# Six late conditioning pieces: from weight-column matmuls on TensorE to multiply-adds on VectorE

## The chip, the cores and the metric

The kernel runs on one core of one Trainium2 chip. The metric is the device time of one launch in microseconds (us). Before the change three runs gave 1612.42, 1619.84 and 1621.44 us, with a median of 1619.84 us. Engines are called as in the profile: PE is TensorE (matmuls; PEld its weight loads), DVE is VectorE, ACT is ScalarE, POOL is GpSimd, SP the engine whose queue issues most of the DMAs.

## The reference, cut to what matters

One decoder layer for 512 tokens of width 1024. A conditioning vector `c` (1024 numbers) is turned into six modulation rows of 1024 numbers, and these scale, shift and gate the two halves of the layer:

```python
mod = jax.nn.silu(c) @ w_ada[l] + b_ada[l]                 # (1, 6*1024)
sh_m, sc_m, g_m, sh_f, sc_f, g_f = jnp.split(mod, 6, axis=-1)
h = modulate(rmsnorm(x, norm_g[l, 0]), sh_m, sc_m)
proj = h @ w_in[l]
a_out = nsa_mixer(...)          # three-branch attention, 8 heads of 64, softmax
c_out = conv_mixer(...)         # depthwise convolution, LayerNorm over channels, swish
x = x + g_m * (jnp.concatenate([a_out, c_out], -1) @ w_out[l])
h = modulate(rmsnorm(x, norm_g[l, 1]), sh_f, sc_f)
x = x + g_f * peer_ffn(h, ...)  # product-key retrieval over 16384 experts
```

The product `silu(c) @ w_ada` is a vector times a 1024 x 6144 matrix. All of it is float32. Only `sh_m` and `sc_m` are needed before the projections; the other rows are needed later.

## The kernel before, in words

The product is cut into twelve pieces of 512 columns (`pc` 0 to 11; piece `pc` belongs to modulation row `pc // 2`). The weights of a piece are two halves (`hf` 0 and 1) of 1 MB, each an SBUF tile `wst` of 128 partitions x 4 x 512: four blocks of 128 rows of `w_ada`. There are three `wst` buffers, which also carry other weights. `cs` holds silu(c) as 128 x 8, and `cs32` the same repeated 32 times along the free side.

Before the change (L207 to L225) a half is four matmuls: block `j` of the weights streams through PE against a 32-column copy of one column of `cs`, into 32 partitions of a PSUM tile of its own block. With `hf` 0 and 1 these accumulate. `mod_fin` lets ACT copy 97 partitions of that PSUM tile into the SBUF tile `rows` (whose last partition holds the bias row, loaded by DMA), and a small matmul against a column that selects partitions 0, 32, 64, 96 and 127 adds the four partial rows and the bias. Its result goes by an ACT copy to `modc` (a column form, pieces 6 to 9) or to `gfbc` (a form broadcast over partitions, pieces 10 and 11).

Pieces 6 to 11 are the late ones. They run inside the attention loop, whose index is `i` from 0 to 17. Iteration `i` computes scores for unit `i` (a query tile of 128 tokens and a pair of heads; four score tiles each, `sc_mm`, L663 on PE and L665 on DVE, which adds the position term and takes the row maximum), exponentials for unit `i - 1` (`sc_exp`, ACT), and for unit `i - 2` the transposes (`turn`, L143 on PE, L698 on ACT) and the products with the values (`values`, L705 and L710 on PE). DVE also scales the exponentials of unit `i - 1` (`weigh`, L685 and L690). Query tile `n` is prepared by `prep` one tile ahead, and a LayerNorm over the convolution's channels is spread over iterations 5, 9, 12 and 13. In the table `mit` the pieces start at the iterations 0, 2, 4, 6, 8 and 10.

The order on DVE in this loop is the order in which the code is written (a manual schedule). The orders on PE, ACT, POOL and SP are set by the framework's list scheduler. Each engine takes its instructions strictly in its order. The score tiles have three PSUM buffers (`s`), the transposes two (`pt`), and one buffer (`x`) serves the pieces, the LayerNorm and `prep` in turn. After the last piece `mod_scale(1)` finishes two rows of `modc`, and `wo_load` starts the loads of the output projection's weights into the same three `wst` buffers; `split` casts the first of them on ACT (`wxhi`, L122) and subtracts on DVE (`wxlo`, L114).

Of the kernel before, what the change touches and what calls it, by code (L numbers as in the profile page):

```python
# [9 lines left out]
F32 = mybir.dt.float32  # L10
# [10 lines left out]
P = 128  # L21
S = 512
# [86 lines left out]
def layer(ctx: ExitStack, tc: tile.TileContext, a, out):  # L109
    nc = tc.nc  # L110
    mult, add, sub = ALU.mult, ALU.add, ALU.subtract

    def tt(o, i0, i1, op):
        return nc.vector.tensor_tensor(out=o, in0=i0, in1=i1, op=op)  # L114

    def act(o, i, f, **k):
        return nc.scalar.activation(o, i, f, **k)  # L117
# [16 lines left out]
    ones = cst[:, C_ONE:C_ONE + P]  # L134
    gbc = {}
    gbc["f"] = const.tile([P, D], F32, name="gfbc")
    modc = const.tile([P, 4, 8], F32, name="modc")
# [7 lines left out]
    with ExitStack() as pre:  # L145
        wpool = pre.enter_context(tc.tile_pool(name="wpool", bufs=1, side="right"))
# [42 lines left out]
        cs = ap_.tile([P, 8], F32, name="cs")  # L189
# [4 lines left out]
        rows = [ap_.tile([P, 512], F32, name=f"rows{k}") for k in range(2)]  # L194
# [6 lines left out]
        def mod_load(pc):  # L201
            was = [wpool.tile([P, 4, 512], F32, name="wst", bufs=3) for _ in range(2)]
            for hf in range(2):
                nc.sync.dma_start(was[hf], a["wada"][pc, hf])
            return was

        def mod_mm(hf, mp, was):  # L207
            for j in range(4):
                nc.tensor.matmul(mp[32 * j:32 * j + 32, :], cs32[:, hf * 4 + j, :], was[hf][:, j, :],
                                 start=hf == 0, stop=hf == 1)  # L210

        def mod_fin(pc, mp, tp, rw):
            act(rw[0:97, :], mp[0:97, :], AF.Copy)
            which, half = pc // 2, pc % 2
            bp = tp()
            if which in (2, 5):
                nc.tensor.matmul(bp, cst[:, C_SEL:C_SEL + 1].to_broadcast([P, P]), rw, start=True, stop=True)
                nc.scalar.copy(gbc["m" if which == 2 else "f"][:, half * 512:(half + 1) * 512], bp)
            else:
                w4 = {0: 0, 1: 1, 3: 2, 4: 3}[which]  # L220
                for cc in range(4):
                    nc.tensor.matmul(bp[:, cc:cc + 1], rw[:, cc * P:(cc + 1) * P], cst[:, C_SEL:C_SEL + 1],
                                     start=True, stop=True)
                (nc.vector.tensor_copy if pc < 4 else nc.scalar.copy)(modc[:, w4, half * 4:half * 4 + 4], bp[:, 0:4])

        def mod_row(pc):
            nc.sync.dma_start(rows[pc % 2][P - 1:P, :], a["bada"][pc:pc + 1, :])

        def mod_both(mp, was):
            for hf in range(2):  # L230
                mod_mm(hf, mp, was)
# [13 lines left out]
        was = {2: mod_load(2), 0: mod_load(0)}  # L245
# [16 lines left out]
        def mod_scale(k, hs=slice(0, 8)):  # L262
            sc = modc[:, 2 * k + 1, hs]
            nc.vector.tensor_scalar(sc, sc, 1.0, None, op0=add)
            tt(sc, sc, ngc[:, k, hs], mult)
# [119 lines left out]
        late = list(range(4, 12))  # L385
# [151 lines left out]
        for n in range(2):  # L537
            for l in range(16):
                nc.tensor.matmul(kcps[:64, n, :], pe[n][:, l:l + 1].to_broadcast([P, 64]), wcmp[:, n, l, :],
                                 start=l == 0, stop=False)  # L540
            for l in range(16):
                nc.tensor.matmul(kcps[:64, n, :], ksb[n][:, 2 * l + 1:2 * l + 1010:16], wcmp[:, n, l, :],
                                 start=False, stop=l == 15)
# [109 lines left out]
        def sc_open(u):  # L653
            u["mx"], u["ng"], u["sm"], u["fc"] = (sb.tile([P, 4], F32, name=n, bufs=4) for n in ("mx", "ngm", "sm", "fc"))
            u["st"], u["pT"] = [], []

        def sc_mm(u, it):
            qt, pr = u["qt"], u["pr"]
            nk, nn = (qt + 1) * P, max((qt + 1) * P, 256)
            h, k = 2 * pr + it // 2, 2 * (it % 2) + pr // 2  # L660
            ps = ps_s.tile([P, S], F32, name="s")
            for q in range(2):
                nc.tensor.matmul(ps[:, :nn], u["o"]["qT"][:, h, :], kst[:, q, k, 0:nn], start=q == 0, stop=q == 1)  # L663
            st = sb.tile([P, S], F32, name="st", bufs=16)
            nc.vector.tensor_tensor_reduce(out=st[:, :nk], in0=ps[:, :nk],  # L665
                                           in1=cst[:, C_BASE + 384 - qt * P:C_BASE + 512],
                                           scale=1.0, scalar=-3e38, op0=add, op1=ALU.max,
                                           accum_out=u["mx"][:, it:it + 1])
            u["st"].append(st)
# [6 lines left out]
        def sc_exp(u, it):  # L676
            nk, h = (u["qt"] + 1) * P, 2 * u["pr"] + it // 2
            st = u["st"][it]
            act(st[:, :nk], st[:, :nk], AF.Exp, scale=float(2.0 ** -(h + 1)),
                bias=u["ng"][:, it:it + 1], accum_out=u["sm"][:, it:it + 1])  # L680
# [11 lines left out]
        def turn(u, it):  # L692
            n = u["qt"] + 1
            pt = ps_t.tile([P, 4, P], F32, name="pt")
            for kb_ in range(n):
                transpose(pt[:, kb_, :], u["st"][it][:, kb_ * P:(kb_ + 1) * P])
            pT = sb.tile([P, 4, P], F32, name="pT", bufs=6)
            nc.scalar.copy(pT[:, :n, :], pt[:, :n, :])  # L698
            u["pT"].append(pT)
# [18 lines left out]
        def x_att():  # L718
            return ps_x.tile([P, S], F32, name="x")

        def tr_att():
            return ps_t.tile([P, 512], F32, name="pt")
# [3 lines left out]
        def wo_load():  # L726
            wos.append(wpool.tile([P, ND, 256], F32, name="wst", bufs=3))
            nc.sync.dma_start(wos[-1], a["wout"][len(wos) - 1])

        mods = {}  # L730

        def mod_get():
            if late:
                pc = late.pop(0)
                mods["next"] = pc, mod_load(pc)
                mod_row(pc)

        def mod_do():
            pc, was = mods.pop("next")
            x = x_att()  # L740
            mod_both(x, was)
            mods["fin"] = pc, x

        def mod_end():
            pc, x = mods.pop("fin")
            mod_fin(pc, x, tr_att, rows[pc % 2])
            if late:
                mod_get()
            else:
                mod_scale(1)  # L750
                for _ in range(3):
                    wo_load()

        late_q, todo = [], {}

        def at_it(i, when, f):
            todo.setdefault((i, when), []).append(f)

        N = 4 * NT
        mit = [0, 2, 4, 6, 8, 10]  # L760
        for i in mit:
            at_it(i, "S", mod_do)
            at_it(i, "E", mod_end)
        L = [5, 9, 12]
        at_it(L[0], "S", ln["mu"])
        at_it(L[0], "E", ln["cen"])
# [2 lines left out]
        at_it(L[2], "S", ln["rep"])  # L769
        at_it(L[2], "E", ln["nrm"])  # L770
        at_it(L[2] + 1, "E", ln["fin"])
        mod_get()
        man = ExitStack()
        man.enter_context(tc.manual_schedule(engines={mybir.EngineType.DVE}))
        us, oo = [], [pre0]
        for i in range(N + 2):
            n, pr = i // 4, i % 4
            A = B = C = None
            if i < N:
                if pr == 0:  # L780
                    oT = ps_o.tile([P, 4, P], F32, name="oT")
                    if n + 1 < NT:
                        oo.append(prep(n + 1, tr_att, x_att))
                        o = oo[-1]
                        at_it(i, "E", o["mul"])
                        todo.setdefault((i + 1, "E"), []).insert(0, o["lo"])
                        at_it(i + 2, "S", o["turn"])
                        at_it(i + 2, "E", o["cmm"])
                        at_it(i + 3, "E", o["cmax"])
                        at_it(i + 4, "E", o["csum"])  # L790
                A = dict(qt=n, pr=pr, o=oo[n], oT=oT)
                sc_open(A)
                us.append(A)
            if 0 <= i - 1 < N:
                B = us[i - 1]
            if 0 <= i - 2 < N:
                C = us[i - 2]
            for k in SL:
                if A:
                    sc_mm(A, k)  # L800
                if B:
                    sc_exp(B, k)
            for f in todo.pop((i, "S"), []):
                f()
            if C:
                for k in SL:
                    turn(C, k)
            if A:
                sc_neg(A)
            if B:  # L810
                weigh(B)
            lq, late_q[:] = list(late_q), []
            if C:
                values(C)
            for f in lq + todo.pop((i, "E"), []):
                f()
            if i < N:
                conv_some(8)
            if i == L[0] - 1:
                conv_some(len(convq))  # L820
# [192 lines left out]
        for h in range(H):  # L1013
# [19 lines left out]
            for t2 in range(2):  # L1033
                ps = psR.tile([P, 2, 2, P], F32, name="sc")
                for k in range(2):
                    t = 2 * t2 + k
                    for c in range(2):
                        nc.tensor.matmul(ps[:, k, c, :], qs[c][:, t * P:(t + 1) * P], kt[:, 2 * h + c, :],
                                         start=True, stop=True)
# [296 lines left out]
    for n in range(NTILE - KL):  # L1336
# [7 lines left out]
        while todo and dma_t < rho * pe_t:  # L1344
            c, f = todo.pop(0)
# [34 lines left out]
```

## Time and profile before

| what | value |
|---|---|
| median of three runs | 1619.84 us (1612.42 to 1621.44) |
| the profiled execution's own time | 1614.99 us |
| its span, from the first to the last instruction | 1613.2 us |
| PE busy over the span | 1560.4 us (97%) |
| DVE busy over the span | 1293.1 us (80%) |
| attention iterations 0 to 11 | 178.98 to 265.64 us of the span |
| DVE busy in these | 52.33 of 86.66 us |
| PE busy in these | 85.58 of 86.66 us |

An iteration is bounded here by the starts of the first of its four score tiles on DVE (L665). A busy share is a sum over instructions; matmuls overlap, so that a full PE is one that never stands empty, not one at its peak. In a timeline row the bracket gives the idle time of the engine before the instruction, and what ended it. The granted clock of PE (PEclk) is 1.00 at 2.4 GHz and 0.50 at 1.2 GHz; values between are averages over a stretch.

### The profile page before, as it was taken

The page shows a single profiled execution, that of the slowest core. Times are in us where ns is not written, and L with a number is a line of the kernel's source. Part 1 is how long each engine was busy: PE and PEld are TensorE (multiplying, and loading weights), DVE is VectorE, ACT ScalarE, POOL GpSimd, SP SyncE. Part 2 cuts the span into 40 slices and gives each one's busy share as a digit, 9 for nine tenths or more (in the row PEclk, how much of TensorE's full clock was granted, in tenths as well). Part 3 has the DMA queues.
Part 4 walks back from the last instruction along what each step waited for, and adds up shares of the span by engine and source line. Part 5 has one row for each costly group of instructions (what it writes and reads, how often), then busy time and mean ns, then how long its engine had stood idle before and what let it go on. Part 6 is the DMA issues. An engine that isn't in the chain of part 4 may idle for free.

```text
span 1613.2 us, 24117 instructions
## 1 busy us (share of the span) xinstructions
PE 1560.4 (97%) x9033; PEld 1361.8 (84%) x9033; DVE 1293.1 (80%) x2590; ACT 755.2 (47%) x1234; POOL 323.3 (20%) x266
## 2 busy tenths in 40 slices
PE   5999998999999999999999999998999999999998
PEld 3779766898889999999999899997897888888887
DVE  4698667578989999988888387786788888878887
ACT  4335558634334544778778433233232333333332
POOL 0000000000002232221222044443454322222210
PEclk9999999999999999999999999999999999999999
DMA  8443242244006877888888989998999999999993
GB/s 316 151 154 123 107 155 79 95 159 152 15 27 206 297 256 252 308 321 311 314 317 283 336 323 337 328 320 312 347 320 346 340 352 352 359 344 350 350 366 143
DMA packets 157166, 416.31 MB, mean 258 GB/s; under 512 B 13036, under 2 KB 76268, under 8 KB 147960
## 3 DMA queue, kind: packets, MB, share of 16 engines
q1 hardware_dynamic: 104048, 236.73, 42.1%
q0 software_dynamic: 36864, 134.23, 23.2%
q10 hardware_dynamic: 16136, 43.79, 7.2%
q8 instruction: 71, 1.16, 0.3%
q14 instruction: 47, 0.39, 0.1%
HBM read 368.25 MB, written 45.88 MB: 257 GB/s over the span
## 4 chain that ended last, share of the span: by engine, by line
PE 71%; DVE 16%; DMA 6%; ACT 4%; issue 3%; SPq 0%; ACTq 0%; DVEq 0%
PE va L1327 8%; PE va L1328 8%; PE va L1326 8%; PE u L1070 7%; PE u L1071 7%; PE u L1072 7%; DVE acc L1179 3%; DVE ulo L114 3%; DVE ldg L1171 3%; DMA ld<-in_uT_dram 3%; DMA ld<-in_vn_dram 2%; ACT vhi L122 2%; PE mm L1026 2%; PE mm L1025 2%; PE mm L1027 2%
## 5 line engine op out<-in xcount | busy, mean ns | idle before, releaser
L1070 PE MATMUL u<-h2hi,uhi 128*128 128x384 f32 x1024 | 350.4, 342 | 7.4 <-ACT act L117 7.2
L1072 PE MATMUL u<-h2hi,ulo 128*128 128x384 f32 x1024 | 346.4, 338 | 4.4 <-DVE ulo L114 4.4
L1071 PE MATMUL u<-h2lo,uhi 128*128 128x384 f32 x1024 | 348.4, 340 | 0.0
L1163 POOL DMA_INDIRECT ldg<-in_un_dram,e_i x128 | 159.8, 1248 | 869.4 <-DVE cand L114 504.6
L1326 PE MATMUL va<-vhi,gshi 128*128 128x512 f32 x756 | 295.9, 392 | 5.3 <-ACT gshi L122 3.4
L1327 PE MATMUL va<-vlo,gshi 128*128 128x512 f32 x756 | 296.7, 393 | 1.6 <-DVE vlo L114 1.5
L1328 PE MATMUL va<-vhi,gslo 128*128 128x512 f32 x756 | 296.4, 392 | 0.0
L114 DVE TENSOR_TENSOR vlo<-ld,vhi 128x1024 fp32r<-128x1024 f32 x126 | 154.3, 1224 | 128.0 <-ACT vhi L122 127.9
L122 ACT CAST vhi<-ld 128x1024 fp32r<-128x1024 f32 x126 | 132.3, 1051 | 229.6 <-issue 164.6
L1163 POOL DMA_INDIRECT ldg<-in_vn_dram,e_i x128 | 161.3, 1260 | 362.8 <-DVE acc L1179 321.6
L1070 PEld LDWEIGHTS u<-h2hi,uhi 128*128 128x128 f32 x1024 | 194.5, 190 | 10.4 <-ACT act L117 8.3
L122 ACT CAST uhi<-ld 128x1024 fp32r<-128x1024 f32 x130 | 137.7, 1060 | 133.4 <-PE u L1071 86.2
L1072 PEld LDWEIGHTS u<-h2hi,ulo 128*128 128x128 f32 x1024 | 194.2, 190 | 5.0 <-DVE ulo L114 5.0
L1071 PEld LDWEIGHTS u<-h2lo,uhi 128*128 128x128 f32 x1024 | 194.5, 190 | 1.3
L114 DVE TENSOR_TENSOR ulo<-ld,uhi 128x1024 fp32r<-128x1024 f32 x130 | 158.5, 1221 | 27.7 <-ACT uhi L122 26.3
L1326 PEld LDWEIGHTS va<-vhi,gshi 128*128 128x128 f32 x756 | 142.8, 189 | 35.6 <-ACT gshi L122 3.7
L1327 PEld LDWEIGHTS va<-vlo,gshi 128*128 128x128 f32 x756 | 142.7, 189 | 31.9 <-DVE vlo L114 3.0
L1328 PEld LDWEIGHTS va<-vhi,gslo 128*128 128x128 f32 x756 | 142.7, 189 | 30.7 <-DVE gslo L114 0.9
L1179 DVE SCALAR_TENSOR_TENSOR acc<-ldg,actg,acc 128x1024 f32<-128x1024 f32 x127 | 162.5, 1279 | 0.0
L1171 DVE SCALAR_TENSOR_TENSOR ldg<-ldg,h2n 128x1024 f32<-128x1024 f32 x128 | 155.9, 1218 | 0.0
L122 ACT CAST gshi<-g 128x384 fp32r<-128x384 f32 x128 | 65.1, 509 | 156.7 <-DVE g L114 156.6
L117 ACT ACTIVATE wb<-mm 128x512 f32<-128x512 f32 x96 | 96.1, 1110 | 47.2 <-PE mm L1134 47.1
(317 smaller groups left out, 2502.8 us busy)
## 6 DMA issues: line engine op xcount, KB each, us to landing
ld<-in_uT_dram SPq DMA_DIRECT2D x128, 512.0 KB
ld<-in_vn_dram SPq DMA_DIRECT2D x128, 512.0 KB
wt<-wd SPq DMA_DIRECT2D x17, 1536.0 KB
wst<-in_wada_dram SPq DMA_DIRECT2D x24, 1024.0 KB
wd<-wb ACTq DMA_DIRECT2D x24, 1024.0 KB
spill<-actw ACTq DMA_DIRECT2D x84, 192.0 KB
sp<-spill SPq DMA_DIRECT2D x21, 768.0 KB
wst<-in_win_dram SPq DMA_DIRECT2D x9, 1024.0 KB
```

The lines of the kernel that those rows point to most:

```text
L114: return nc.vector.tensor_tensor(out=o, in0=i0, in1=i1, op=op)
L117: return nc.scalar.activation(o, i, f, **k)
L122: nc.scalar.copy(hi, src)
L1070: nc.tensor.matmul(ps, hi[:, d, :], h2hi[:, d, :TD], start=d == 0, stop=False)
L1071: nc.tensor.matmul(ps, hi[:, d, :], h2lo[:, d, :TD], start=False, stop=False)
L1072: nc.tensor.matmul(ps, lo[:, d, :], h2hi[:, d, :TD], start=False, stop=d == ND - 1)
L1163: nc.gpsimd.indirect_dma_start(out=gst[-1], out_offset=None, in_=a["un" if kind == "u" else "vn"], in_offset=bass.IndirectOffsetOnAxis(ap= ...
L1171: nc.vector.scalar_tensor_tensor(g, g, 1.0, h2n, op0=mult, op1=mult, accum_out=actg[:, k:k + 1])
L1179: nc.vector.scalar_tensor_tensor(acc, g, actg[:, k:k + 1], acc, op0=mult, op1=add)
L1326: nc.tensor.matmul(vac[t][k], ghi[:, ts_], vhi[:, ks], start=f, stop=False)
L1327: nc.tensor.matmul(vac[t][k], ghi[:, ts_], vlo[:, ks], start=False, stop=False)
L1328: nc.tensor.matmul(vac[t][k], glo[:, ts_], vhi[:, ks], start=False, stop=l)
```

## The change: what it does, and the diff

The matmuls of the six late pieces go. Each of the twelve halves becomes four `scalar_tensor_tensor` instructions on DVE: a 128 x 512 block of weights times the per-partition scalar `cs[:, 4*hf+k]`, added to `rows`. After eight of them `rows` holds 128 partial rows, one per partition; beforehand a POOL memset clears it, and the bias row is loaded into its last partition by the same DMA as before. PE then sums over the partitions with a column of ones (four matmuls with one column, or one with 128), and ACT copies the result as before; the ACT copy of the 97 partitions is gone. A queue `modq` holds the steps: four adds, then the load of a further half, after every second half also the sum; one step is taken after each score tile up to iteration 4, two from iteration 5 on. Three halves are loaded ahead.

```diff
-        def mod_do():
-            pc, was = mods.pop("next")
-            x = x_att()
-            mod_both(x, was)
-            mods["fin"] = pc, x
...
+            pc, hf = halves.pop(0)
+            wa, rw = wpool.tile([P, 4, 512], F32, name="wst", bufs=3), rows[pc % 2]
+            nc.sync.dma_start(wa, a["wada"][pc, hf])
+            if hf == 0:
+                nc.gpsimd.memset(rw, 0.0)
                 mod_row(pc)
...
+            def add_in(k):
+                nc.vector.scalar_tensor_tensor(rw, wa[:, k, :], cs[:, 4 * hf + k:4 * hf + k + 1], rw, op0=mult, op1=add)
+
+            modq.extend([lambda k=k: add_in(k) for k in range(4)])
+            if hf == 1:
+                modq.append(lambda: mod_end(pc, rw))
+            modq.append(mod_get)
+
+        def mod_end(pc, rw):
+            which, half = pc // 2, pc % 2
+            bp = tr_att()
+            if which in (2, 5):
+                nc.tensor.matmul(bp, ones, rw, start=True, stop=True)
+                nc.scalar.copy(gbc["m" if which == 2 else "f"][:, half * 512:(half + 1) * 512], bp)
             else:
+                for cc in range(4):
+                    nc.tensor.matmul(bp[:, cc:cc + 1], rw[:, cc * P:(cc + 1) * P], ones[:, 0:1], start=True, stop=True)
+                nc.scalar.copy(modc[:, {3: 2, 4: 3}[which], half * 4:half * 4 + 4], bp[:, 0:4])
+            if pc == 11:
                 mod_scale(1)
                 for _ in range(3):
                     wo_load()
...
-        mit = [0, 2, 4, 6, 8, 10]
-        for i in mit:
-            at_it(i, "S", mod_do)
-            at_it(i, "E", mod_end)
...
+        for _ in range(3):
+            mod_get()
...
+                mod_some(1 if i < 5 else 2)
```

The order of the instructions moves on three engines. DVE in iterations 9 and 10 (`st` is a score tile, `mx` its row maximum, `ngm` the maximum scaled for the exponentials; `rows_99` and `rows_100` are the two `rows` buffers):

```order
 L665 ISA st,mx<-s,cst 128x384
 L665 ISA mx 128x1
+L745 SCALAR_TENSOR_TENSOR rows_99<-wst,cs,rows_99 128x512
 L665 ISA st,mx<-s,cst 128x384
 L665 ISA mx 128x1
+L745 SCALAR_TENSOR_TENSOR rows_100<-wst,cs,rows_100 128x512
 L665 ISA st,mx<-s,cst 128x384
 L665 ISA mx 128x1
+L745 SCALAR_TENSOR_TENSOR rows_100<-wst,cs,rows_100 128x512 x2
 L665 ISA st,mx<-s,cst 128x384
 L665 ISA mx 128x1
+L745 SCALAR_TENSOR_TENSOR rows_100<-wst,cs,rows_100 128x512
```

The adds stand between the score tiles of an iteration, so that the later score tiles, the scaling and everything behind them on DVE come after up to seven adds of the same iteration (iteration 8 has seven; these are the five of iteration 9).

PE in iterations 1 to 3 (`s` are score products, L222 and L760 the sums of piece 6, `qr` the transposes of the next query tile):

```order
 L705 MATMUL oT<-pc,vbl 128x128
-L663 MATMUL s<-kst,qT 128x256
-L222 MATMUL pt<-cst,rows_99 128x1 x4
-L663 MATMUL s<-kst,qT 128x256 x5
-L209 MATMUL x<-wst,cs_97 32x512 x8
-L143 MATMUL pt<-cst,qr 128x128
-L663 MATMUL s<-kst,qT 128x256 x2
-L143 MATMUL pt<-cst,qr 128x128 x7
+L663 MATMUL s<-kst,qT 128x256 x16
+L760 MATMUL pt<-cst,rows_99 128x1 x4
+L143 MATMUL pt<-cst,qr 128x128 x8
```

The eight matmuls of a piece are gone from between the score products, and the sum of a piece comes later, behind the score products of iteration 2.

ACT in iteration 12, where a LayerNorm's activation (`y<-y,cvec`) needs another table of functions, before the change:

```order
L698 COPY pT<-pt 128x384 x2
L117 ACTIVATE st,sm<-st,ngm 128x512 x4
L117 ACT_TABLE_LOAD
L117 ACTIVATE y<-y,cvec 128x512 x4
L641 CAST hhi<-y 128x512 x4
L471 COPY pc<-pt 128x256
L698 COPY pT<-pt 128x384
L117 ACT_TABLE_LOAD
L117 ACTIVATE st,sm<-st,ngm 128x512
```

The same place after it:

```order
L117 ACTIVATE st,sm<-st,ngm 128x512
L698 COPY pT<-pt 128x384
L117 ACTIVATE st,sm<-st,ngm 128x512 x2
L117 ACT_TABLE_LOAD
L117 ACTIVATE y<-y,cvec 128x512 x4
L641 CAST hhi<-y 128x512 x4
L471 COPY pc<-pt 128x256
L117 ACT_TABLE_LOAD
L117 ACTIVATE st,sm<-st,ngm 128x512
```

The fourth exponential of unit 12 has moved behind the LayerNorm's block and its two table loads.

## Rows read from the trace of the kernel before

**Rows 1.** Windows by iteration: length, each engine's busy us (instructions), PEclk, DMA share, GB/s.
```profile
core 0: us, PE busy (x) PEld busy (x) DVE busy (x) ACT busy (x) POOL busy (x), PEclk, DMA share, GB/s
...
189.84:198.14 8.30, 8.30 (x55) 6.72 (x55) 3.93 (x20) 4.94 (x24) 0.00 (x0) 0.79 0.36 146
...
254.55:265.64 11.09, 11.09 (x90) 8.20 (x88) 7.53 (x21) 9.40 (x24) 0.00 (x0) 1.00 0.24 88
sum 86.66, PE 85.58 PEld 58.81 DVE 52.33 ACT 56.75 POOL 0.00; mean PE 7.13 PEld 4.90 DVE 4.36 ACT 4.73 POOL 0.00
```

**Rows 2.** Waits on DVE, iterations 0 to 11: waiter, waited for, total, times, longest.
```profile
DVE st L665 <- PE s L663: 26.9, 14, 4.5
DVE fc L685 <- ACT st L117: 4.3, 2, 2.3
DVE rv L627 <- ACT rv L117: 1.4, 1, 1.4
```

**Rows 3.** The same windows, only the pieces' matmuls (L209): the sum.
```profile
sum 86.66, PE 15.80 PEld 2.87; mean PE 1.32 PEld 0.24
```

**Rows 4.** Groups on ACT and PE: busy us, mean ns, idle before.
```profile
L117 ACT ACTIVATE rows<-x 97x512 f32<-97x512 f32 x6 | 3.5, 590 | 6.3 <-PE x L209 6.3
L222 PE MATMUL pt<-cst,rows 128*128 128x1 f32 x32 | 4.1, 249 | 0.0
```

**Rows 5.** DVE, the convolution's multiply-adds (L379) and a two-operand subtraction: start, length, operation.
```profile
L379 DVE SCALAR_TENSOR_TENSOR y<-up,dww,y x120: 637/732/751, 62.6 to 174.6; 128x482 f32<-128x482 f32 x4, 128x483 f32<-128x483 f32 x4, 128x484 f32<-128x484 f32 x4, 128x485 f32<-128x485 f32 x4
...
109.46 10.41 DVE L379 SCALAR_TENSOR_TENSOR y<-up,dww,y 128x505 f32<-128x505 f32 x16
...
211.55 2.47 DVE L114 TENSOR_TENSOR y<-y,x 128x512 f32<-128x512 f32 x4
```

**Rows 6.** Timeline of DVE: two waits for score tiles, in iterations 3 and 11.
```profile
194.22 0.29 DVE L665 CUSTOM_DVE_ANT_0 st<-s,cst 128x128 f32<-128x128 f32 x1 [4.09 <-PE s L663]
...
259.45 0.56 DVE L665 CUSTOM_DVE_ANT_0 st<-s,cst 128x384 f32<-128x384 f32 x1 [3.39 <-PE s L663]
```

**Rows 7.** PE busy and PEclk in stretches of 3 us.
```profile
192.00:195.00 3.00, 3.00 (x23) 0.89 0.26 107
195.00:198.00 3.00, 3.00 (x16) 0.54 0.01 3
198.00:201.00 3.00, 3.00 (x22) 1.00 0.00 0
...
240.00:243.00 3.00, 3.00 (x15) 0.50 0.00 0
243.00:246.00 3.00, 3.00 (x13) 0.57 0.00 0
```

**Rows 8.** Groups on PE from 239 to 246 us, then from 247 to 257 us.
```profile
L663 PE MATMUL s<-kst,qT 128*128 128x384 f32 x8 | 3.3, 527 | 0.0
L143 PE MATMUL pt<-cst,st 128*128 128x128 f32 x8 | 2.1, 424 | 0.0
...
L663 PE MATMUL s<-kst,qT 128*128 128x384 f32 x8 | 1.9, 363 | 0.0
L143 PE MATMUL pt<-cst,st 128*128 128x128 f32 x12 | 1.7, 277 | 0.0
```

**Rows 9.** Side conditions: POOL group, DMA window, then DVE and ACT timeline around iteration 12.
```profile
L198 POOL MEMSET rows<- 128x512 f32 x2 | 1.0, 524 | 0.3 <-POOLq L1369 0.3
...
183.00:186.00 3.00, 3.00 (x29) 1.00 1.01 415
...
262.20 2.28 DVE L114 TENSOR_TENSOR wxlo<-wst,wxhi 128x2048 fp32r<-128x2048 f32 x1
...
277.06 0.17 DVE L685 RECIPROCAL fc<-sm 128x4 f32<-128x4 f32 x1
...
280.39 0.72 ACT L117 ACTIVATE st<-st,ngm 128x512 f32<-128x512 f32 x1
```

More of the change, by code (lines that the diff above doesn't have):

```diff
@@ L728, in wo_load @@
             nc.sync.dma_start(wos[-1], a["wout"][len(wos) - 1])
-        mods = {}
+        modq, halves = [], [(pc, hf) for pc in late for hf in range(2)]
+        del late[:]
         def mod_get():
-            if late:
-                pc = late.pop(0)
-                mods["next"] = pc, mod_load(pc)
-                mod_row(pc)
-        def mod_do():
-            pc, was = mods.pop("next")
-            x = x_att()
-            mod_both(x, was)
-            mods["fin"] = pc, x
[L744 to L748, printed above, removed]
-            else:
+            if not halves:
+                return
+            pc, hf = halves.pop(0)
[3 more added lines that the diff above has]
+                nc.gpsimd.memset(rw, 0.0)
+                mod_row(pc)
+            def add_in(k):
[10 more added lines that the diff above has]
+                nc.scalar.copy(gbc["m" if which == 2 else "f"][:, half * 512:(half + 1) * 512], bp)
+            else:
+                for cc in range(4):
+                    nc.tensor.matmul(bp[:, cc:cc + 1], rw[:, cc * P:(cc + 1) * P], ones[:, 0:1], start=True, stop=True)
+                nc.scalar.copy(modc[:, {3: 2, 4: 3}[which], half * 4:half * 4 + 4], bp[:, 0:4])
+            if pc == 11:
                 mod_scale(1)
@@ L752, in mod_end, with mod_some @@
                     wo_load()
+        def mod_some(n):
+            for _ in range(n):
+                if modq:
+                    modq.pop(0)()
         late_q, todo = [], {}
@@ L771, in layer @@
         at_it(L[2] + 1, "E", ln["fin"])
-        mod_get()
+        for _ in range(3):
+            mod_get()
         man = ExitStack()
```

## The prediction

> **What bounds the kernel now.** I read the windows first, cut at the attention iterations, because the change touches iterations 0 to 11 alone; what lies before and behind keeps its instructions and moves as a block with the loop's end. In these 86.66 us PE stands empty for about 1 us, while DVE is busy for 52.33 us [rows 1]. So before the change PE sets the pace here, and the next view, who waits for whom, says the same from the other side: DVE waits 26.9 us for score products, 4.3 us for exponentials and 1.4 us for a root, together 32.6 us [rows 2]. DVE's work with the small gaps between dependent instructions is therefore 86.66 - 32.6 = 54.1 us. Third I looked at what the pieces cost PE: 15.80 us over the loop [rows 3]. Last came the timeline, for where DVE's waits lie: not spread evenly, but one of 3 to 4 us in an iteration in which PE has much between two score tiles, as in iterations 3 and 11 [rows 6].
>
> **What the change removes.** PE loses the 15.80 us of piece matmuls [rows 3]. ACT loses six copies of 0.59 us, 3.5 us in all [rows 4]; ACT is busy 56.75 of 86.66 us [rows 1] and is not the bound, so I count this at nothing. The summing matmuls keep their shapes (L222 before, 4.1 us [rows 4], L760 after). PE's own need falls from about 86 to about 70 us.
>
> **What it adds.** DVE gets 12 halves x 4 = 48 multiply-adds over 128 x 512. The trace has the same operation, with the same accumulation on its own output: the convolution's taps. One lasts 0.73 us in the middle of 120, but neighbours overlap, and sixteen in a row take 10.41 us, which is 0.65 us each [rows 5]. Lower bound: a subtraction of 128 x 512, four of which take 2.47 us, hence 0.60 us with the overlap taken off [rows 5]; upper bound: the longest tap alone, 0.751 us. I take 0.65, since it is the same operation: 48 x 0.65 = 31.2 us (28.8 to 36.0).
>
> So DVE's work becomes 54.1 + 31.2 = 85.3 us in a loop that took 86.66 us. This is the main step of the forecast: the waits of DVE are just large enough to hold the adds (32.6 against 31.2), and the pace passes from PE to DVE. If every wait were filled, the loop would be 1.4 us shorter, no more, whatever PE has won.
>
> **What isn't filled.** The adds stand at fixed places in DVE's order, after the score tiles, and the waits are where PE has a long piece of work between two score products. In iteration 3 DVE waits 4.09 us for its second tile [rows 6], and only one add stands before it; the sum of piece 6, about 1 us of PE, comes off this place since it now runs ahead of the transposes. 4.09 - 0.65 - 1 leaves about 2.5 us. Iteration 11 has no add at all, and its PE order is as before: of 3.39 us I keep 3.0. The other 25.1 us of waits fall in iterations with three to seven adds (2.0 to 4.6 us) and I count them as filled; the two waits for exponentials go, as the adds give ACT the time. So 5.5 us remain. Bounds: 0 us, and at the other end 3 us in each of iterations 3, 7, 9 and 11, where PE has the preparation of a query tile or the LayerNorm's sums between two score products: 12 us (the longest single wait before is 4.5 us [rows 2]).
>
> **Where the clock comes in.** In the stretch from 195 to 198 us PE was granted 0.54 and from 240 to 246 us about 0.5, which is the 1.2 GHz level, though PE was never empty there; behind the first of them it was back at 1.00, the 2.4 GHz level [rows 7]. At the low level a score product takes 527 ns instead of 363 and a transpose 424 instead of 277, 1.5 times as long [rows 8]. Without the pieces PE will stand empty for about a quarter of the loop (70 of some 93 us are its need). The Trainium skill, "TensorE: Matmul & The Clock Gate", Part 1, says that the throttled state is the default and that activity releases it; by that rule the removal makes every remaining matmul of the loop slower rather than only removing work, and the trace agrees in so far as the level does change within this loop, while no run yet shows the loop without the pieces. In rows: at the two places that stay PE-bound PE works for about 4.4 us before the awaited tile (iteration 3, 189.84 to 194.22) and 4.9 us (iteration 11, 254.55 to 259.45) [rows 1, 6]; at 1.5 times that costs 2.2 and 2.5 us. Bounds 0 and 4.7 us; I take half, 2.4 us, since one of the two (iteration 3) already was partly slow before at 0.79 [rows 1].
>
> **Side costs, taken at nothing.** Six POOL memsets of 0.52 us [rows 9] run on an idle engine. The clearing, the bias row and the first add of piece `pc + 2` wait for PE's sum of piece `pc`, but 11 steps of the queue lie between, over an iteration. A load of 1 MB takes 2.5 us at 415 GB/s [rows 9] and has eight adds and at least one iteration of lead; if that cover were gone, an add would block DVE and the score tiles behind it for 1 to 3 us each time. `wxlo`, 2.28 us on DVE [rows 9], moves from iteration 11 into iteration 10 before the last score tile; it now waits for a load that starts when an add of iteration 9 frees the buffer and for an ACT cast, which I see in time by about 1 us (up to 2 us lost if not). In iteration 12 the fourth exponential comes behind the LayerNorm's block. Before, the scaling of that unit stood on DVE at 277.06 and the first exponential after the block at 280.39 [rows 9]; DVE will so wait about 3 us there. It costs nothing or up to 1 us, since the transposes of that unit come only in iteration 14, two iterations behind its scores.
>
> **Sum.** 85.3 + 5.5 + 2.4 = 93.2 us against 86.66, that is +6.5 us. On the profiled execution's 1614.99 us this is 1621.5 us. That execution lies below the median of the runs (1619.84) and above the lowest (1612.42); the mean of these four executions is 1617.2, and I set the forecast on it: 1617.2 + 6.5, or 1624 us.
>
> **Rivals.** *DVE and PE in turn, slower.* Each iteration takes the longer of the two engines, and PE runs at the low clock through the loop. Place: the score tiles behind the transposes in iterations 3, 7, 8 and 11; price 85.3 + 12 = 97.3 us, plus up to 4.7 us for the clock: +11 to +15 us, say +13, 1630 us. It decides if PE is at the low level in more than half of the loop or if more than 9 us of DVE's waits for score products stay. For it: waits of up to 4.5 us at single places, three score buffers only. Against it: PE's work drops by a sixth, so that it can run ahead by its order. *The adds fill every wait, no loss.* DVE is then full and the loop takes 83 to 87 us: -4 to +1 us, 1616 us. For it: 32.6 against 31.2 us; against it: iteration 11 without adds. *PE's gain arrives, faster.* A loop shorter by 8 us would need 78.6 - 54.1 = 24.5 us for 48 adds, 0.51 us each, below the 0.60 of the simpler subtraction; 1608 us. Nothing in the rows speaks for it. *The change stalls on its own inputs*, the adds waiting for loads or for the cleared `rows`: six stalls of 2 us, 1636 us; the lead of one iteration speaks against it.
>
> **How the numbers follow.** About 0.5% (8 us) is what a measurement of this kernel can tell from no change. Forecast (+1 to +8 us): 0.46, own range 1618 to 1627. No loss: 0.09. Engines in turn: 0.36. Own inputs: 0.04. Faster: 0.05. So within 0.5%: 0.46 + 0.09 = 0.55; slower: 0.40; faster: 0.05. The range: below, 28.8 us of adds without any wait, 82.9 us, -3.8 us, 1613; above, adds at 0.751 us (36.0 instead of 31.2) on top of the engines in turn with the whole clock term, 106.8 us, +20 us, 1637.
>
> **What would show it.** Right: DVE busy about 84 us over iterations 0 to 11, its waits for score products down from 26.9 to 5 to 9 us, an add about 0.74 us long at steps of 0.65, idle time on PE that DVE ends, and the first score tile of iteration 12 near 272 instead of 265.64. Clock step: PEclk near 0.5 in iterations 3 and 11. Wrong: adds that take under 0.6 us, waits of DVE for `wst` or `rows`, or a changed stretch behind iteration 13.

## The result and the profile after

The changed kernel takes 1639.71 us (median of 4 runs, 1635.73 to 1642.41), the kernel before on the same chip 1618.93 us (4 runs, 1612.42 to 1621.44). The ratio is 1.0138, with a 95% interval of 1.0097 to 1.0179: slower by about 21 us (16 to 29), where the forecast was 6.5 us (1624 us). The time lies above the range given, whose top was 1637 us.

The windows of after, cut at its iterations as in [rows 1]: iterations 3, 6 and 11, then the whole loop (first score tile of iteration 0 to that of iteration 12).

```profile
core 0: us, PE busy (x) PEld busy (x) DVE busy (x) ACT busy (x) POOL busy (x), PEclk, DMA share, GB/s
...
195.11:204.65 9.54, 9.49 (x62) 7.18 (x61) 5.82 (x23) 5.53 (x27) 0.00 (x0) 0.94 0.22 75
...
221.24:228.97 7.73, 6.26 (x27) 5.79 (x28) 7.59 (x24) 2.29 (x6) 0.53 (x1) 0.50 0.37 136
...
269.84:278.46 8.62, 8.60 (x84) 7.12 (x82) 5.42 (x21) 7.17 (x22) 0.00 (x0) 1.00 0.13 51
...
180.78:278.46 97.68, 80.58 (x484) 61.40 (x482) 83.62 (x260) 55.03 (x169) 2.10 (x4) 0.81 0.39 141
```

The loop took 97.68 us instead of 86.66. DVE is now busy nearly all the time in iteration 6 (7.59 of 7.73 us), but not in iterations 3 and 11 (5.82 of 9.54, 5.42 of 8.62), where PE is busy throughout. Before, the same loop had a mean granted clock of 0.94:

```profile
178.98:265.64 86.66, 85.58 (x587) 58.81 (x585) 52.33 (x211) 56.75 (x176) 0.00 (x0) 0.94 0.39 147
```

The waits of after in the loop, DVE's and then PE's longest (columns as in [rows 2]):

```profile
DVE st L665 <- PE s L663: 12.4, 6, 3.5
...
PE s L663 <- DVE mx L665: 13.7, 11, 4.7
```

All of PE's waits in the loop of before:

```profile
PE pt L143 <- ACT rows L117: 0.8, 1, 0.8
PE x L209 <- DVE y L114: 0.3, 1, 0.3
```

DVE's waits fell from 32.6 us [rows 2] to 12.4. PE, which waited about 1 us in all before, waits 13.7 us for DVE to have read a score tile: each engine now waits for the other in some iterations. The adds, answering to [rows 5], as a group and as a pair in the timeline of iteration 7:

```profile
L745 DVE SCALAR_TENSOR_TENSOR rows<-wst,cs,rows 128x512 f32<-128x512 f32 x48 | 35.9, 748 | 0.4
...
230.31 1.54 DVE L745 SCALAR_TENSOR_TENSOR rows<-wst,cs,rows 128x512 f32<-128x512 f32 x2
```

Behind the loop, ScalarE at the LayerNorm's last block and the step of DVE that waited for it:

```profile
285.37 1.28 ACT L117 ACT_TABLE_LOAD   x1
286.67 2.93 ACT L117 ACTIVATE y<-y,cvec 128x512 f32<-128x512 f32 x4
...
291.95 1.28 ACT L117 ACT_TABLE_LOAD   x1
293.25 0.72 ACT L117 ACTIVATE st<-st,ngm 128x512 f32<-128x512 f32 x1
...
294.09 0.18 DVE L685 RECIPROCAL fc<-sm 128x4 f32<-128x4 f32 x1 [4.34 <-ACT st L117]
```

The fourth exponential of iteration 12 now comes behind the block and both table loads, and DVE waits 4.34 us for it. Before, the same scaling came at 277.06, ahead of the block's end [rows 9].

All profiled executions in one table, in us; the experiments behind the names follow. *Loop*: as above. *Waits*: all waits of DVE in it, for PE and others. *Tail*: from the loop's end to the first matmul of the output projection. *Rest*: the span without loop and tail. Each row is a single execution: for e2_both, e3_even and e4_half it was the slowest of their four, for e6_cut and e9_place the fastest of theirs.

| kernel | loop | clock in it | DVE's waits | loop less waits | tail | rest |
|---|---|---|---|---|---|---|
| before | 86.66 | 0.94 | 32.6 | 54.1 | 39.3 | 1487.3 |
| after | 97.68 | 0.81 | 12.4 | 85.3 | 42.0 | 1497.2 |
| after, second execution (e10_after) | 97.70 | 0.81 | 12.4 | 85.3 | 42.0 | 1485.8 |
| after, third execution (e11_after) | 106.86 | 0.71 | 21.9 | 85.0 | 42.7 | 1492.9 |
| e5_act | 100.97 | 0.80 | 15.7 | 85.3 | 43.3 | 1487.6 |
| e6_cut | 79.58 | 0.94 | 26.2 | 53.4 | 39.3 | 1487.0 |
| e6_cut, second execution (e12_cut) | 94.76 | 0.77 | 41.0 | 53.8 | 39.3 | 1489.6 |
| e7_adds | 104.85 | 0.87 | 19.8 | 85.1 | 42.2 | 1488.3 |
| e8_fill | 100.16 | 0.86 | 14.1 | 86.1 | 42.7 | 1485.8 |
| e9_place | 98.58 | 0.79 | 11.1 | 87.5 | 44.0 | 1486.2 |
| e1_thin | 88.49 | 0.79 | 27.5 | 61.0 | 43.7 | 1488.6 |
| e2_both | 111.44 | 0.80 | 26.3 | 85.1 | 42.5 | 1489.2 |
| e3_even | 104.07 | 0.70 | 21.6 | 82.5 | 39.9 | 1491.9 |
| e4_half | 95.41 | 0.86 | 27.0 | 68.4 | 41.9 | 1491.6 |

### The profile page after: what moved, and what is told of

It is laid out like the page before. It is cut to its first block, busy times and chain, and to the rows that moved or that the text cites. A ratio compares the mean times of both kernels' runs of the same rounds, so it can differ in the third digit from the quotient of the medians.

```text
span 1636.9 us, 23987 instructions
## 1 busy us (share of the span) xinstructions
PE 1559.5 (95%) x8937; PEld 1367.1 (84%) x8937; DVE 1323.9 (81%) x2638; ACT 753.6 (46%) x1228; POOL 326.2 (20%) x272
## 4 chain that ended last, share of the span: by engine, by line
PE 69%; DVE 17%; DMA 7%; ACT 4%; issue 4%; SPq 0%; ACTq 0%; DVEq 0%
PE va L1343 8%; PE va L1344 8%; PE va L1342 8%; PE u L1086 7%; PE u L1087 7%; PE u L1088 7%; DMA ld<-in_uT_dram 4%; DVE acc L1195 3%; DVE ldg L1187 3%; DVE ulo L114 2%; PE mm L1042 2%; PE mm L1041 2%; PE mm L1043 2%; DMA ld<-in_vn_dram 2%; ACT vhi L122 2%
## 5 line engine op out<-in xcount | busy, mean ns | idle before, releaser
L1086 PE MATMUL u<-h2hi,uhi 128*128 128x384 f32 x1024 | 350.3, 342 | 15.2 <-ACT act L117 15.0
```

The lines of the kernel that those rows point to most:

```text
L1086: nc.tensor.matmul(ps, hi[:, d, :], h2hi[:, d, :TD], start=d == 0, stop=False)
```

## The experiments

The theory that I began with, A, was that DVE's work sets the loop and that the adds alone make it longer; its rival was PE's clock, and later that both engines work in turn.

### e1_thin: adds of 16 columns instead of 512

```diff
-  scalar_tensor_tensor(rw, wa[:, k, :], cs[...], rw, ...)
+  scalar_tensor_tensor(rw[:, 0:16], wa[:, k, 0:16], cs[...], rw[:, 0:16], ...)
```

> The changed kernel, but each multiply-add covers 16 of its 512 columns; loads, clearing, sums and their order stay (the modulation rows come out incomplete). I compare three stretches: the loop from the first score tile of iteration 0 to that of iteration 12 (86.66 us before, 97.68 us changed), the tail from there to the first matmul of the output projection (39.3 and 42.0 us), and the rest from the first matmul over the experts' keys to the end (1151.5 and 1159.6 us). Theory A, DVE's work sets the loop: an add falls from about 0.69 to about 0.12 us, DVE's work from 85.3 to about 58 us, PE becomes the bound again without the pieces: loop 72 to 80 us, launch 10 to 15 us below the kernel before plus what the rest does. Rival B, it isn't the adds' length but what hangs on them (late sums, clearing, loads): loop over 90 us.

Measured: 1622.05 us against 1614.43, ratio 1.0049 (1.0028 to 1.0070); loop 88.49 us.

```profile
179.94:268.43 88.49, 79.52 (x471) 62.56 (x471) 59.41 (x260) 52.98 (x165) 2.37 (x4) 0.79 0.43 155
...
188.00:191.00 3.00, 3.00 (x16) 0.50 0.79 273
191.00:194.00 3.00, 3.00 (x16) 0.50 0.19 77
194.00:197.00 3.00, 3.00 (x16) 0.50 0.00 0
```

Theory A falls as I had put it: DVE has 24 us less to do than in after, PE 15.8 us less than in before, and the loop still is longer than before. It lies between the two expectations (up to 80 us and over 90 us). DVE waits 25.8 us for score products, and PE has the low clock for long stretches although it is busy in each of those shown.

### e2_both: the adds, and four piece matmuls per half, spread

```diff
 def add_in(k):
+    if k == 0:
+        xk = x_att()
+        for j in range(4):
+            matmul(xk[32 * j:32 * j + 32, :], cs32[:, hf * 4 + j, :], wa[:, j, :], start=True, stop=True)
```

> The changed kernel, with the removed matmuls put back beside the adds: at the first add of each half PE multiplies the half into the x buffer as before, and nobody reads the result. If the low clock of PE (0.50 in about 30 of 98 us of the changed loop) is what keeps 12.4 us of DVE waiting, the 512-column matmuls bring the clock back to 0.95 or more and the loop stays at 94 to 98 us in spite of 15.8 us more PE work. If the two engines simply take turns, the loop grows to 102 to 110 us. If DVE alone set it and PE had room to spare, it stays within 1 us of 97.7 with the clock no matter.

Measured: 1642.71 us, ratio 1.0162 (1.0132 to 1.0191); loop 111.44 us at a clock of 0.80, above what either reading gave. Putting the matmuls back in twelve small groups did not bring the clock back. So I could not take it that the pieces' work as such holds the clock.

### e3_even: one add behind every score tile

```diff
-  mod_some(1 if i < 5 else 2)    # every step of the queue takes a place
+  mod_some(1)                    # only an add takes a place; the steps behind it run along
```

> The changed kernel with one add after every score tile of iterations 0 to 11 (48 in 48 places); sums and loads cost no place of their own. In ACT's order all four exponentials of unit 12 then stand ahead of the LayerNorm's table load, as before the change. Theory: the 12 pairs of neighbouring adds (1.45 us instead of 2 x 0.66) go, 1.5 us, and adds stand where DVE waits in iterations 3 and 11: loop 93 to 97 us. Tail: if the fourth exponential behind the table loads made the 4.3 us wait, the tail falls from 42.0 to 39 to 40 us; if not, it stays at 42.

Measured: 1631.46 us, ratio 1.0095 (1.0066 to 1.0125). The tail came back to 39.9 us, since in this order all four exponentials of iteration 12 stand ahead of the table load. The loop's expectation, 93 to 97 us, failed: 104.07 us, at a clock of 0.70. DVE's own work fell by 2.8 us (82.5 against 85.3), since no two adds are neighbours. This execution (1637.61 us) lies above the median, and after itself has loops of 97.68 to 106.86 us at clocks of 0.81 to 0.71; so whether an even spread shortens the loop is not shown.

### e4_half: pieces 6, 8 and 10 on TensorE, 7, 9 and 11 on VectorE

```diff
+  for i in (0, 4, 8):
+      at_it(i, "S", mod_pe)        # piece matmuls, as before the change
+      at_it(i, "E", mod_pe_end)
-  mod_some(1 if i < 5 else 2)
+  mod_some(1 if i in (2, 3, 6, 7, 9, 10) else 0)
```

> Half of the change: pieces 6, 8 and 10 on PE as before (at iterations 0, 4 and 8), pieces 7, 9 and 11 as adds on DVE in iterations 2, 3, 6, 7, 9 and 10, four in each. PE's need falls by 7.9 us from 86, DVE's work rises from 54.1 to 54.1 + 16 = 70 us, so neither is full. Theory A gives a loop of 79 to 83 us, below both kernels, and a tail of 42 us (three exponentials ahead of the table load): launch 1 to 5 us below the kernel before. Rival, the engines take turns whatever the balance: loop 87 to 92 us and a launch between the two kernels.

Measured: 1628.03 us, ratio 1.0078 (1.0056 to 1.0100); loop 95.41 us. Half the adds cost 8.8 us of loop where theory A gave a gain; that is also above the 87 to 92 us of the rival. DVE waited 23.0 us for score products, where it had waited 26.9. Of its 24 adds (68.4 - 54.1 = 14.3 us), 5.6 us went into waits (27.0 in all against 32.6), and 8.8 us came on top. PE, with half of the pieces gone, was busy for 86.82 us at a clock of 0.86, no less than before (85.58 at 0.94).

### e5_act: the LayerNorm's last block an iteration later

```diff
-  at_it(L[2], "E", ln["nrm"])
-  at_it(L[2] + 1, "E", ln["fin"])
+  at_it(L[2] + 1, "S", ln["nrm"])
+  at_it(L[2] + 2, "E", ln["fin"])
```

> After, with one step moved: the LayerNorm's last block on ScalarE is issued an iteration later, so that the fourth exponential of iteration 12 stands ahead of it, as before the change. The loop keeps its order, so it is a second look at after's loop. Both theories: first score tile of iteration 0 to that of iteration 12 in 96 to 99.5 us, mean granted clock about 0.81. Tail (iteration 12 to the first matmul of the output projection): 39.0 to 40.0 us if the 4.3 us wait behind the LayerNorm's block is what made it 42.0 in after; 42 if it is not. Time over before: +10 to +13 us in the first case on the loop and the tail alone.

Measured: 1635.77 us against 1614.68, ratio 1.0146 (1.0115 to 1.0177); loop 100.97, tail 43.3 us. The tail's expectation failed: the block and its two table loads then stood ahead of all four exponentials of the next unit, and DVE waited 5.3 us there instead of 4.3. Moving the block moves the wait. The loop, the same program as after's up to iteration 12, was 3.3 us longer than in after's first execution and above the 99.5 us expected, all of it in DVE's waits (15.7 against 12.4 us).

### e6_cut: before, with piece matmuls and copies of 16 columns

```diff
-  mod_both(x, was)
+  # for each of the eight blocks, hf 0 and 1, j 0 to 3:
+  matmul(x[32 * j:32 * j + 32, 0:16], cs32[:, hf * 4 + j, :], was[hf][:, j, 0:16], ...)
-  act(rw[0:97, :], mp[0:97, :], AF.Copy)
+  act(rw[0:97, 0:16], mp[0:97, 0:16], AF.Copy)
```

> The kernel before with the matmuls of the six pieces (and their copies) cut from 512 to 16 columns, with no adds on VectorE: neither the work removed nor the work added. Clock theory (without the pieces TensorE is granted the low clock for long stretches and that eats what it won): loop 80 to 88 us, mean granted clock 0.75 to 0.88. Rival (TensorE's gain is real and only the adds on VectorE take it back): loop 70 to 78 us and granted clock 0.92 or more; the time would be 9 to 16 us below before.

Measured: 1612.81 us against 1614.68, ratio 0.9994 (0.9973 to 1.0015): no change, though 13 us of PE's busy time were gone at the same clock and DVE had nothing added. The profiled execution, the fastest of ten (1607.68 us), had a loop of 79.58 us at a clock of 0.94, 7.1 us below before; that is the clock of the rival and a loop between the two expectations. The other executions reached 1621.56 us, with a lower mean clock over the span (0.988 in the fastest, 0.977 at 1620.05 and at 1616.15). So the same program was run and profiled once more:

> The kernel before with the piece matmuls cut to 16 columns, once more: its ten times lay between 1607.7 and 1621.6 us, the fast ones with a mean granted clock near 0.987 and the slow ones near 0.978; the first look was one of the fast (loop 79.6 us). If the clock inside the loop makes this difference, a look with a mean clock under 0.98 shows a loop of 85 to 92 us with stretches at 0.50; if the difference lies behind the loop, the loop is 79 to 81 us again.

The second execution (1625.46 us, on another chip, where before had 1614.73) shows the other end: its loop is longer than the 85 to 92 us expected, with stretches at 0.50 as expected. The loop's row and DVE's waits in it, of the first:

```profile
180.44:260.02 79.58, 72.36 (x590) 57.73 (x589) 51.66 (x211) 55.78 (x178) 0.00 (x0) 0.94 0.44 167
...
DVE st L665 <- PE s L663: 22.4, 12, 5.5
```

and of the second, with two of its stretches:

```profile
181.68:276.44 94.76, 87.77 (x590) 70.38 (x589) 51.99 (x212) 56.46 (x178) 0.00 (x0) 0.77 0.37 140
...
222.00:225.00 3.00, 3.00 (x17) 0.50 1.07 344
...
261.00:264.00 3.00, 3.00 (x14) 0.50 0.01 5
...
DVE st L665 <- PE s L663: 37.3, 13, 8.0
```

The same 590 matmuls were busy 15.4 us longer, and the loop was 15.2 us longer, with DVE's own work the same (53.4 and 53.8 us). What the two traces show to differ is the clock; that the chip has no part in it is not shown, though the ten times of the first chip spread by 14 us too. The loop without the pieces lies 7 us below before's one profiled loop or 8 us above it, and the times come out at no change.

### e7_adds: before, with 48 adds beside its piece matmuls

```diff
+  # after each score tile, at the places that after gives them
+  scalar_tensor_tensor(jk[:, 0, :], jk[:, 1, :], cs[:, 0:1], jk[:, 0, :], op0=mult, op1=add)
```

> The kernel before with its piece matmuls, and beside them 48 adds of 128x512 on VectorE (on a tile of their own, not used) at the places where after has them: the work added, and none removed. Clock theory: granted clock 0.90 or more as in before, TensorE needs its 85.6 us, VectorE 85.3, and the loop is 95 to 102 us. Rival (VectorE's adds make TensorE wait, and that alone brings the clock down): granted clock about 0.80, loop 104 to 112 us as in the run with both and the matmuls spread.

Measured: 1636.74 us, ratio 1.0140 (1.0121 to 1.0160), the same as the change itself. Loop 104.85 us at 0.87. DVE's waits in it:

```profile
DVE st L665 <- PE s L663: 11.8, 6, 4.7
DVE wxlo L114 <- ACT wxhi L122: 6.9, 1, 6.9
DVE fc L685 <- ACT st L117: 1.1, 1, 1.1
```

6.9 us of it are a stall of their own: in this order the split of the first output weight waits for its cast. Less this stall the loop would be 98 us, an estimate, with waits for score products of 11.8 us: after's loop, though PE kept the 15.8 us that the change takes away. The loop as measured lies in the range of the rival, less the stall in that of the clock theory; the clock, 0.87, fits neither. By this one execution, taking the matmuls off PE was worth nothing beside the adds.

### e8_fill: after, with 16 dense matmuls where TensorE stood empty

```diff
+  if i in (0, 1, 4, 5):
+      matmul(xf, ones, gbc["m"][:, 0:512], start=True, stop=True)   # nobody reads xf
   mod_some(1 if i < 5 else 2)
```

> After, with 16 more matmuls of 128x512 that nobody reads, one behind each score tile of iterations 0, 1, 4 and 5, where TensorE stood empty in after ahead of the stretches at the low clock. Clock theory (the clock falls because TensorE stands empty there): granted clock 0.9 or more from 185 to 200 us and from 215 to 230 us, loop 90 to 95 us although TensorE has some 10 us more to do. Rival (in turn: whatever TensorE gets more comes on top): loop 99 to 106 us, clock as in after.

Measured: 1631.76 us, ratio 1.0129 (1.0077 to 1.0180); loop 100.16 us at 0.86. PE and its clock in this run, where after had 0.50, 0.69 and 0.50 in the stretches from 186, 219 and 225 us:

```profile
186.00:189.00 3.00, 3.00 (x17) 1.00 0.66 276
189.00:192.00 3.00, 1.49 (x11) 0.96 0.00 0
195.00:198.00 3.00, 3.00 (x14) 0.50 0.10 39
...
219.00:222.00 3.00, 3.00 (x13) 1.00 0.86 303
225.00:228.00 3.00, 1.97 (x16) 1.00 0.21 33
```

The clock stayed up in iterations 4 to 7, and DVE's wait in iteration 7 was gone. In iteration 3 the clock fell all the same, and there DVE waited 5.86 us; ahead of it, in iteration 2, which has no fillers, PE was busy for 1.49 of 3 us. So half of the clock theory holds: in iteration 7 the clock was up and the wait gone. But the fillers did not shorten the loop, which lies in the range of the rival: the waits for score products came to 14.1 us in all, against 12.4 in after.

### e9_place: after, with the adds where DVE waited before

```diff
-  mod_some(1 if i < 5 else 2)
+  mod_some(plan.get((i, k), 0))   # none in iterations 1 and 2, 6 at (3, 0), 7 in iteration 7, 7 in 11, ...
```

> After, with its 48 adds at other places of VectorE's order: none in iterations 1 and 2, six behind the first score tile of iteration 3, seven ahead of the third of iteration 7, and so on where VectorE waited for score products in the kernel before. Theory in turn (the loop is VectorE's 85 us plus the waits for score products in the iterations with much TensorE work, 3, 7, 8 and 11): these waits fall from 12.4 us to 4 to 6 us and the loop to 89 to 92 us, time over before +5 to +9 us. Rival (TensorE at the low clock sets the loop, whatever VectorE's order): waits of 11 us or more, loop 96 to 102 us.

Measured: 1638.41 us, ratio 1.0157 (1.0134 to 1.0181); loop 98.58 us. Its waits:

```profile
DVE st L665 <- PE s L663: 7.3, 6, 3.8
DVE wxlo L114 <- ACT wxhi L122: 2.1, 1, 2.1
DVE fc L685 <- ACT st L117: 1.7, 1, 1.7
```

The waits for score products fell by 5.1 us, less than the 6 to 8 of the theory. Two other waits of together 3.8 us and 2.2 us more of DVE's own work (87.5 against 85.3) took all of it; the longest wait is now at the first tile of iteration 7. The loop lies in the range of the rival, the waits in that of neither. These places alone don't make the change pay.

### e10_after and e11_after: after again, twice

Nothing is edited.

> After once more, unchanged: a second look at its loop. In turn: VectorE's work is 85 to 86 us again and only the waits for score products vary, by the clock in iterations 3, 7, 8 and 11: loop 97 to 102 us, the tail to the output projection's first matmul 42 us, the stretch from the first up-projection to the end 1150 to 1156 us (1159.6 in the first look would be chance). Rival (the 8 us behind the output projection in the first look belong to the change): 1158 to 1161 us again.

> After a third time, as the second look: loop 97 to 102 us and last stretch 1150 to 1156 us, or 1158 to 1161 us if the change slows it.

Measured: 1627.26 and 1644.23 us, one run each, on the same chip in one session, where before had 1614.73. The loop in the second execution and in the third:

```profile
180.30:278.00 97.70, 80.59 (x484) 61.50 (x482) 83.59 (x259) 55.01 (x169) 2.10 (x4) 0.81 0.40 141
```

```profile
180.80:287.66 106.86, 89.75 (x484) 69.83 (x482) 83.31 (x259) 55.59 (x169) 2.10 (x4) 0.71 0.36 128
```

DVE's long waits in it, again in the second and in the third, in iterations 3, 7, 8 and 11:

```profile
199.14 0.29 DVE L665 CUSTOM_DVE_ANT_0 st<-s,cst 128x128 f32<-128x128 f32 x1 [3.55 <-PE s L663]
233.77 0.43 DVE L665 CUSTOM_DVE_ANT_0 st<-s,cst 128x256 f32<-128x256 f32 x1 [2.38 <-PE s L663]
246.57 0.56 DVE L665 CUSTOM_DVE_ANT_0 st<-s,cst 128x384 f32<-128x384 f32 x1 [1.84 <-PE s L663]
273.41 0.56 DVE L665 CUSTOM_DVE_ANT_0 st<-s,cst 128x384 f32<-128x384 f32 x1 [3.02 <-PE s L663]
```

```profile
201.95 0.29 DVE L665 CUSTOM_DVE_ANT_0 st<-s,cst 128x128 f32<-128x128 f32 x1 [5.86 <-PE s L663]
239.83 0.42 DVE L665 CUSTOM_DVE_ANT_0 st<-s,cst 128x256 f32<-128x256 f32 x1 [5.29 <-PE s L663]
255.35 0.56 DVE L665 CUSTOM_DVE_ANT_0 st<-s,cst 128x384 f32<-128x384 f32 x1 [4.93 <-PE s L663]
283.07 0.56 DVE L665 CUSTOM_DVE_ANT_0 st<-s,cst 128x384 f32<-128x384 f32 x1 [3.90 <-PE s L663]
```

and PE with its clock ahead of the second of these waits, in the second execution and in the third:

```profile
228.00:231.00 3.00, 3.00 (x20) 0.67 0.24 39
231.00:234.00 3.00, 3.00 (x31) 1.00 0.81 320
```

```profile
228.00:231.00 3.00, 3.00 (x16) 0.50 0.85 322
231.00:234.00 3.00, 3.00 (x14) 0.50 0.24 33
234.00:237.00 3.00, 3.00 (x19) 0.50 0.80 317
237.00:240.00 3.00, 3.00 (x16) 0.50 0.03 8
```

One program, one order, the same work of DVE (85.3 and 85.0 us), and loops of 97.70 and 106.86 us. The four waits grow by 2.31, 2.91, 3.09 and 0.88 us, together 9.2, and that is the loop's difference; where PE has the low clock for longer, the tile that DVE waits for comes later. The expectation for the third execution (97 to 102 us) was too narrow.

The last stretch that the expectation names took 1148.7 and 1155.4 us (1150 to 1156 expected if chance), so the 1159.6 of the first execution doesn't belong to the change as such. The rest was 1485.8 and 1492.9 us, against 1497.2 in the first and 1487.3 in before. Most of that difference can be seen in the trace of the first, far behind the loop: ScalarE waits for a load of the experts' weights, and PE for ScalarE.

```profile
1119.80 1.04 ACT L122 CAST uhi<-ld 128x1024 fp32r<-128x1024 f32 x1 [16.11 <-DMA ld<-in_uT_dram]
1121.29 0.69 PE L1086 MATMUL u<-h2hi,uhi 128*128 128x384 f32 x1 [10.71 <-ACT act L117]
```

The longest wait of this kind is 5.3 us in before, 2.1 in the second execution of after and 7.6 in the third.

## Why the prediction was wrong

**What bounds the kernel now**: right for before. PE sets the pace there; e6_cut, whose loop is 79.6 us where PE keeps its clock, shows that PE's work was worth 7 us in that execution, with nothing added to DVE.

**What the change adds**: right. Loop less waits rose from 54.1 to 85.3 us, by 31.2 us, the 48 x 0.65 forecast; DVE's 85.3 us came out in three further executions (85.3, 85.0, 85.3). That it fits to the tenth is partly luck: two neighbouring adds take 1.45 us to the start of the next step where a single one takes 0.66, and e3_even, without such pairs, came to 28.4 us, 0.59 for each add.

**What isn't filled, and the clock term**: this is the step that failed. I put 5.5 us of waits and 2.4 us of clock on top of 85.3, 7.9 in all; measured were 12.4, 12.4, 15.7 and 21.9 us. By place, in the first execution: iteration 11 kept 2.99 where I had 3.0. Iteration 3 kept 4.9 us (1.35 and 3.51) where I had 2.5: the sum of piece 6, taken off there as 1 us, did not go but moved ahead of the iteration's first tile, and DVE now waits 1.35 us there. This is PE's row of the sum, at a clock of 0.50; the transposes of the next query tile stand behind it:

```profile
190.97 1.87 PE L760 MATMUL pt<-cst,rows 128*128 128x1 f32 x8
```

Iterations 7 and 8 kept 2.36 and 1.87; of these waits I had said "I count them as filled". The longest wait before was in iteration 7:

```profile
223.52 0.42 DVE L665 CUSTOM_DVE_ANT_0 st<-s,cst 128x256 f32<-128x256 f32 x1 [4.48 <-PE s L663]
```

It has five adds, but only three of them ahead of the awaited tile, 0.66 and 1.45 us; 4.48 less these is 2.37 us, nearly what was measured. So the step that I took for iteration 3 would have given this wait too. In iteration 8 five of the seven adds stand ahead of the awaited tile and do not fill the wait, since the LayerNorm's 32 one-column sums (L621, 4.00 us on PE), in iteration 9 before, now stand there.

The clock I had priced at two places, at half. The sign given for it, 0.5 in iterations 3 and 11, did not come in the first execution (0.94 and 1.00). Between e10_after and e11_after the waits at all four places grow as the clock falls, by 9.2 us in one program. Behind this step stands the picture itself: I took DVE's 32.6 us of waits as room for 31.2 us of adds. In after an add ahead of a wait delays the reading of a score tile, PE then waits for the tile's buffer (13.7 us, none before), and its next product comes later. In e4_half, where 8.8 of 14.3 us of adds came on top, PE waited only 2.4 us for buffers; there its work at the lower clock is the likelier reason, which no run separates.

**What the change removes**: PE lost the 15.80 us of matmuls, but its busy time in the loop fell only from 85.58 to 80.58 us, and in the third execution it rose to 89.75, as what remained ran at 0.81 and 0.71 instead of 0.94. The 70 us that I gave as PE's need hold only at the clock of before. The Trainium skill, "TensorE: Matmul & The Clock Gate", Part 1, says that activity releases the throttle; by that, the fillers of e8_fill should bring the clock back. The trace agrees from 207 to 240 us, where the clock was up, and does not show it in iteration 3, where PE was busy in every stretch and had 0.50.

**Side costs**: the loads, the memsets and the clearing cost nothing, as said: no wait of DVE for `wst` or `rows` is in the loop of after, and `wxlo` did not wait there. The exponential behind the LayerNorm's block, "nothing or up to 1 us", cost 2.8 us of tail in the first two executions (42.0 against 39.3) and 3.5 in the third; e3_even, where it stands ahead, gets back to 39.9.

**The rivals.** "DVE and PE in turn" was the one that came: it named the four iterations and 97.3 us plus up to 4.7, and decided on more than 9 us of waits for score products. Measured were 97.7, 97.7, 101.0 and 106.9. Its time, 1630 us, was still 10 us short. I gave it 0.36 and should have preferred it: DVE's waits were single places of up to 4.5 us [rows 2], and one or two adds per tile (0.66 to 1.45 us) do not fill such a wait.

**The sum.** Loop, in four executions with that order: +11.0, +11.0, +14.3 and +20.2 us, +14.1 in the mean; tail +2.8 to +3.5. Together some +17 us, within the +16 to +29 of the runs but below their middle (+21). The remaining 4 us lie in the rest of the span, 1490.9 us in the mean of these four against 1487.3 in before's one; but it differs by up to 11 us between executions of one program (1485.8 to 1497.2), much of it in the wait for a load shown above, so it is open whether the change has a part in it. Nor did any run hold the full clock through the loop with all adds on DVE. How much of the 12.4 us would go with it is open; the 2.99 us of iteration 11 stood at 1.00.

No version beat both kernels: with the adds on DVE none came below before, and e6_cut, which only leaves work out, came out equal to it.

## What to carry to other kernels

Idle time of an engine that works in turn with another is not room: before you fill it, ask at each wait whether the added work stands between the two tiles that the wait separates, and whether the other engine will then wait for a buffer. Price what stays on TensorE at the clock that it will have without the removed matmuls, at every place where another engine waits for it, and give the range both levels. Where a loop's length less its waits is constant over experiments, as the 85 us here, the rest of the question is which waits remain, and a second and third execution of the same program show how far these vary by themselves.

## What the runs showed of the hardware

- One program on one chip had a loop of 97.70 and of 106.86 us with mean granted clocks of 0.81 and 0.71 (e10_after, e11_after), and another, on two chips, of 79.58 and 94.76 us with 0.94 and 0.77 (e6_cut and its second execution, e12_cut).
- PE can be busy in every stretch of 3 us and have 0.50 for a long time: from 228 to 240 us in the third execution of after, with transposes, score, compressed-key and value products, and again in e1_thin from 188 to 197 us.
- A multiply-add of 16 columns in e1_thin is far from free, at 231 ns against 748 for 512 columns:

```profile
L745 DVE SCALAR_TENSOR_TENSOR rows<-wst,cs,rows 128x16 f32<-128x16 f32 x48 | 11.1, 231 | 0.4
```

A thirty-second of the columns has a third of the duration, and 0.14 us as its share of the loop ((61.0 - 54.1) / 48).
